# The second state scan issued in pieces between output tiles and weight slots, with GpSimd's two-operand work moved around it

## The chip, the core and the metric

The program runs on one core of a Trainium2 chip. The metric is device microseconds of one execution. The kernel before took 2566.79 us, the median of 3 runs (2566.29 to 2571.04). Engines are named as the profile names them: PE is TensorE, DVE is VectorE, ACT is ScalarE, POOL is GpSimd, SP is SyncE, which issues most DMAs.

## What is computed

One inference step of a two-layer decoder over 304 token columns (a prompt of 16 meta and 256 new tokens, and 8 sample sequences of 4 tokens). Layer 0 is a gated short convolution and a squared-ReLU MLP. Layer 1 is a state space mixer with a gated linear unit (GLU), and another MLP. Only the mixer of layer 1 is touched here:

```python
h_re, h_im = associative_scan(...)          # h[t] = A h[t-1] + B u[t], complex, diagonal
y = einsum(C_re, h_re) - einsum(C_im, h_im) + D * u
g = gelu(y)
out = (g @ w_a) * sigmoid(g @ w_b)          # 2048 x 2048 each
```

## The kernel before, in words

All large products are split into two rounded parts for accuracy: each weight slot of 256 rows x 512 columns is loaded as `raw`, ACT copies it to a rounded part `whi` (L64), and DVE or POOL subtracts to get the rest `wlo` (L66). Three matmuls per pair of tiles follow (L194, L195, L196). A slot is 24 such matmuls. `WeightStream.take` prepares slots two ahead of the one in use; `whi` and `wlo` have 3 buffers each, `raw` has 4. Each slot names the engine that does its L66, "dve" or "pool".

The mixer works on chunks of four tokens. There are 76 chunks (68 of the prompt, 8 of the samples) and 16 channel tiles, in two parts: tiles 0 to 5 (TP1) and tiles 6 to 15 (TP2). For each part the inputs to the states are formed (`m1_run`), then `st_scan` runs the recurrence over the prompt's chunks on DVE, then each tile's output is formed (`y_run`): `st_t` and `st_y` (PE, L1098 and L1107), ACT's copy `vy` (L1112), the transposes of `st_c` (PE, L1123), gelu (ACT, L1126), the rounded part of `g` (ACT, L1129) and the rest (`gt_lo`, POOL, L1130).

`st_scan(1)`, the second scan, has on DVE, in this order:

- 15 steps of four 320-column instructions (L1041, L1042, L1045, L1047), side by side for four blocks of 17 chunks,
- one last step in two shapes, and three carries between blocks (L1060 to L1065),
- six corrections of four 640-column instructions (L1077 to L1080): three for the first half of the states (tiles 6 to 10), then three for the second (tiles 11 to 15).

`st_scan_samples` advances the sample sequences with 8 two-operand instructions on POOL (L1090 to L1093).

The order of the program around it is fixed by the code: the engines' queues are filled in program order. Before: `st_scan(1)` whole, then `y_run(TP1)`, during which slots 0 to 2 are prepared, then four GLU groups of three slots each on tiles 0 to 5 (`group(K1, ...)`, 12 slots, below called slots 0 to 11), then `st_scan_samples(1)`, `y_run(TP2)`, `fin_copy(1)` (POOL gathers the final states, L1220) and the rest of the GLU ("phase 2" below; its first slots are 12, 13, 14). In phase 2, PE transposes the final states (`fin_tr`, L1240) after its fourth slot. The lower parts of slots 0 to 14 are POOL's.

Of the kernel before, what the change touches and what calls it, by code (L numbers as in the profile page):

```python
# [16 lines left out]
P = 128  # L17
D = 2048
DFF = 8192
NT = D // P           # 16 channel tiles  # L20
NK = 76               # 68 prompt chunks of 4 tokens, then 8 sample sequences of 4 tokens
NP = 68
NS = 8
NM = 4                # chunks of meta tokens
NL = NK - NM          # 72 chunks that live on after the state space mixer
N0 = 4 * NK           # 304 columns: column j * 76 + k holds token j of chunk k
N1 = 4 * NL           # 288
# [8 lines left out]
RATE = (2, 0, 0, 2, 3, 3)  # L36


class WeightStream:
    """Weights come in slots of 256 rows x 512 columns; each is split exactly into two float32r parts."""  # L40
# [37 lines left out]
def build(ctx, tc, I, O, dbg=None):  # L78
# [50 lines left out]
    for n, mg in glu[:NPHASE1]:  # L129
        wgroup(I[n][0], K1, mg * 512, "pool")  # L130
# [15 lines left out]
    def later(fn, delay=1, front=False):  # L146
        """front: what frees an accumulator goes before all else"""
        if front:
            i = 0
            while i < len(tasks) and tasks[i][2]:  # L150
                i += 1
            tasks.insert(i, (W.idx + delay, fn, True))
        else:
            tasks.append((W.idx + delay, fn, False))
# [9 lines left out]
    def pop_tasks(n):  # L164
        """second halves of what began at the last call, then one accumulator, then other work"""
        run_pend()
        if tasks and tasks[0][2] and tasks[0][0] <= W.idx:
            tasks.pop(0)[1]()
            if heavy[0]:
                return  # L170
        k = 0
        i = 0
        while i < len(tasks) and k < n:
            if not tasks[i][2] and tasks[i][0] <= W.idx:
                tasks.pop(i)[1]()
                k += 1
            else:
                i += 1
# [7 lines left out]
    def group(kts, rhs, n, rate=1, fast=False):  # L186
        """512 columns of a product: four accumulators; the last one comes late in the first slot"""
        ps = [psum() for _ in range(4)]

        def mm(m, kk, si, hi, lo):  # L190
            xh, xl = rhs(kts[si + kk])
            o = ps[m][:, :n]
            wh, wl = hi[:, kk, m * P:(m + 1) * P], lo[:, kk, m * P:(m + 1) * P]
            T.matmul(out=o, lhsT=wh, rhs=xh, start=si == 0 and kk == 0, stop=False)  # L194
            T.matmul(out=o, lhsT=wh, rhs=xl, start=False, stop=False)  # L195
            T.matmul(out=o, lhsT=wl, rhs=xh, start=False, stop=si + 2 >= len(kts) and kk == 1)  # L196

        for si in range(0, len(kts), 2):
            while si == 0 and len(tasks) > 3 and tasks[3][2]:
                tasks.pop(0)[1]()  # L200
            run_pend()
            hi, lo = W.take()
            if si + 2 >= len(kts):
                order = [(m, kk) for m in range(4) for kk in range(2)]
            else:
                order = [(m, kk) for kk in range(2) for m in range(4 if si else 3)]
                if si == 0:
                    order += [(3, 0), (3, 1)]
            for m, kk in order[:4]:
                mm(m, kk, si, hi, lo)  # L210
            pop_tasks(rate)
            for m, kk in order[4:]:
                mm(m, kk, si, hi, lo)
            if len(tasks) > 5 or fast:
                pop_tasks(rate)
            else:
                run_pend()
            if bg:
                f = bg[0]
                if hasattr(f, "__next__"):  # L220
                    if next(f, bg) is bg:
                        bg.pop(0)
                else:
                    bg.pop(0)
                    if f is not None:
                        it = f()
                        if hasattr(it, "__next__"):
                            bg.insert(0, it)
        return ps

# [21 lines left out]
    def warm_pe(n):  # L252
        """keeps the tensor engine's clock up over a short wait"""
        ps = psum1()
        for _ in range(n):
            T.matmul(out=ps[:, :P], lhsT=ones, rhs=ones, start=True, stop=True)
# [46 lines left out]
    def cols(ap, n):  # L303
        """the last n / 4 chunks of each of the four token rows"""
        v = ap.rearrange("p (j k) -> p j k", j=4)
        return v[:, :, v.shape[2] - n // 4:]
# [29 lines left out]
    def norm_tile(x, t, n, base, eng=None):  # L336
        """square sums and the scaled, split operand of the next product"""
# [4 lines left out]
    def rsqrt_from(ps, s, y, out, then=None):  # L342
        """1 / sqrt(mean + eps): root and reciprocal, then a Newton step"""
# [92 lines left out]
    d_b = dp.tile([2, 64, P, 16], F32, name="d_b")         # ri, p, g, c  # L436
    d_c = dp.tile([2, 64, P, 4, 16], F32, name="d_c")      # ri, p, g, tau, c'
    d_m1 = dp.tile([NT, 2, 64, 4, 2, 64], F32, name="d_m1")  # tile, g2, (j c), q, ri, p
    d_m2 = dp.tile([NT, 2, 64, 4, 2, 64], F32, name="d_m2")  # tile, g2, p, q, ri, (i c')
    d_u = dp.tile([D, N0], F32, name="d_u")  # L440
    d_t = dp.tile([4, 16, P, 4, 16], F32, name="d_t")      # j, c, g, i, c'

    def prep_tasks():
# [27 lines left out]
        def vexp(x, out, ta, tb, tcc):  # L471
            """exp by reduction to |r| <= ln2/2 and a polynomial; x is kept"""
# [15 lines left out]
        # slots of nat: 0 lr, 1 li, 2 log_step, 3 dt, 4..7 temps, 8+2n.. A^(n+1), 16+2n.. E_n  # L488
# [22 lines left out]
        def cmul(o, a, b):  # L511
            """complex product of slot pairs"""
# [29 lines left out]
        def t_wnorm():  # L542
            """the mixer's input weights join B and D"""
# [115 lines left out]
        # local kernels K_tau = Re(C A^tau Bbar), with D on the diagonal of K_0  # L659
# [88 lines left out]
    def taps(t, i):  # L748
        """the convolution over time, scaled by the norm of what it will meet"""
# [87 lines left out]
    def mlp(x, n, base, last_ev):  # L837
        """last_ev(t): what follows once a tile of the residual stream is final"""
# [86 lines left out]
    def u_in(ta, tb):  # L925
        """partition (g2, j, c) of U: token j of a chunk, channel c of every other state group"""
# [30 lines left out]
    def st_m1(t):  # L957
        """inputs to the chunk states, by chunk"""
# [18 lines left out]
    def st_m1t(t):  # L977
        """the same by state, into the scan"""
# [26 lines left out]
    def powers(n):  # L1005
        """A^(4(n+1)) of the block scan's corrections"""
# [14 lines left out]
    def st_scan(pi):  # L1021
        """chunk states: four blocks of 17 chunks side by side, then the carries between them"""
# [13 lines left out]
        def step(items):  # L1036
            """items: previous states, new states (holding the inputs), blocks"""
# [11 lines left out]
        for k in range(1, LBK - 1):  # L1049
            step([(bv[:, :, k], bv[:, :, k + 1], NBK)])  # L1050
        step([(bv[:, 0:3, LBK - 1], bv[:, 1:4, 0], 3), (bv[:, 3:4, LBK - 1], sh[:, NK:NK + 1], 1)])
# [3 lines left out]
        def carry(b):  # L1055
            """i times the carry into block b; the next carry += A^68 times it"""
# [9 lines left out]

        for b in range(1, NBK):
            carry(b)
        n = LBK - 1
        for qa, qb in QCUT[pi]:  # L1070
# [3 lines left out]
            for b in range(1, NBK):  # L1074
# [5 lines left out]
                V.tensor_tensor(out=hb, in0=hb, in1=t2, op=ALU.add)  # L1080

    def st_scan_samples(pi):
        sh = ssm["SH"][pi]
        q0, nq = qrange(pi)
        x, y = (s_[:, 0:NS * nq].rearrange("p (s q) -> p s q", s=NS) for s_ in ssm["st"])
# [29 lines left out]
    def g_at(t):  # L1115
        """rounded and remaining parts of tile t of the mixer's activations, over two buffers"""
        return gh[t // 8][:, t % 8, :], gh[t // 8][:, 8 + t % 8, :]

    def st_c(t):
# [10 lines left out]
        G.tensor_tensor(out=gt_lo, in0=gt[:, :N1], in1=gt_hi.bitcast(F32), op=ALU.subtract)  # L1130
# [5 lines left out]
    # layer 0's MLP, with the transposes of the finished tiles running under its last products  # L1136
# [26 lines left out]
    # rstd in the layout of U: partition (g2, j, c), column k  # L1163
# [24 lines left out]
    st_scan(0)  # L1188
# [3 lines left out]
    st_scan(1)  # L1192
# [9 lines left out]
    def y_run(ts):  # L1202
        ts = list(ts)
        for n, t in enumerate(ts):
# [5 lines left out]
            if 0 < n <= LOOK + 1:  # L1210
                W.prep_to(W.idx + n)
        st_c(ts[-1])

    y_run(TP1)
# [3 lines left out]
    def fin_copy(pi):  # L1218
        q0, nq = qrange(pi)
        G.tensor_copy(out=fin[0].rearrange("p (s r q) -> p s r q", s=9, r=2)[:, :, :, q0:q0 + nq],  # L1220
                      in_=ssm["SH"][pi][:, NK:85])
# [6 lines left out]
    for gi in range(NPHASE1):  # L1228
        ps = group(K1, rhs_g, N1, 0)
        for i in range(4):  # L1230
            S.activation(out=part[:, gi * 4 + i, :], in_=ps[i][:, :N1], func=AF.Copy)
    st_scan_samples(1)
# [15 lines left out]

    fin_copy(1)
# [3 lines left out]
    # gated linear unit  # L1253
# [108 lines left out]
```

## Time and profile before

| What | Value |
|---|---|
| Runs | 2566.29, 2566.79, 2571.04 us |
| Profiled execution, its span | 2566.6 us |
| PE busy | 2458.1 us (96%) |
| DVE busy | 1488.9 us (58%) |
| ACT busy | 967.7 us (38%) |
| POOL busy | 402.1 us (16%) |
| Granted PE clock, mean | 0.982 of full speed |

PE is the busiest engine by far; its 40 slices are full nearly everywhere, with a dip in slice 24 of 40, where the mixer's second part is. The table is an average over stages with different limits. The change lies in the stretch from 1400 to 1600 us of the span, where DVE is at 9 tenths for two slices.

### The profile page before, as it was taken

Reading aid. Unit: us, or ns where it says so; the run is one execution under the profiler, and the core shown is the slowest. Engines: PE = TensorE matmul, PEld = TensorE weight load, DVE = VectorE, ACT = ScalarE, POOL = GpSimd, SP = SyncE. Lnnn points to the kernel's source line nnn. Section 1 sums busy time; section 2 is a strip of 40 time slices with the busy share of each in tenths; the row PEclk is TensorE's granted clock in tenths of the full one; section 3 lists DMA queues with packets and bytes.
Section 4 is the critical chain, followed back from the end, with each engine's and each line's share of the span. In section 5 each row is a group of like instructions: output and inputs, shape, how many; then the busy total and the mean of one; then the engine's idle time right before and its main releaser. Section 6 shows DMA issues by size and latency. Waiting matters only on the chain.

```text
span 2566.6 us, 43303 instructions
## 1 busy us (share of the span) xinstructions
PE 2458.1 (96%) x18078; PEld 2433.9 (95%) x18078; DVE 1488.9 (58%) x1994; ACT 967.7 (38%) x1229; POOL 402.1 (16%) x459
## 2 busy tenths in 40 slices
PE   6999999999989999999989859999999999999998
PEld 5999999998889999999988759999999999999998
DVE  4654556677566675544546992556555545555555
ACT  4333334432334233333324524444333333333334
POOL 2000001025324870000045342000000000000000
PEclk9999999999999999999999979999999999999999
DMA  6555555555656776555569524555555555555554
GB/s 149 156 157 157 160 160 170 158 160 144 164 147 195 221 209 214 158 167 170 159 150 184 153 89 133 165 165 164 166 163 172 161 169 166 165 169 166 165 165 111
DMA packets 256353, 418.17 MB, mean 163 GB/s; under 512 B 64484, under 2 KB 68260, under 8 KB 255980
## 3 DMA queue, kind: packets, MB, share of 16 engines
q1 hardware_dynamic: 248448, 389.62, 52.1%
q0 software_dynamic: 7648, 25.73, 4.8%
q8 instruction: 142, 2.33, 0.4%
q14 instruction: 55, 0.45, 0.0%
q10 hardware_dynamic: 60, 0.05, 0.0%
HBM read 392.71 MB, written 22.63 MB: 162 GB/s over the span
## 4 chain that ended last, share of the span: by engine, by line
PE 59%; DVE 6%; DMA 1%; ACT 0%; issue 0%; SPq 0%; DVEq 0%; ACTq 0%
PE ps L194 19%; PE ps L196 19%; PE ps L195 19%; DVE ssm_tb L1042 1%; PE ps L1107 1%; DVE ssm_tb L1041 1%; DVE ssm_big L1047 1%; DMA raw<-in_mlp_w_down 1%; DVE wlo L66 1%; PE px L684 1%; DVE ssm_big L1045 1%; DMA ssm_xr<-d_u 0%; PE ps L1326 0%; PE ps L1098 0%; ACT whi L64 0%
## 5 line engine op out<-in xcount | busy, mean ns | idle before, releaser
L66 DVE TENSOR_TENSOR wlo<-raw,whi 128x1024 fp32r<-128x1024 f32 x689 | 891.6, 1295 | 931.6 <-ACT whi L64 931.0
L64 ACT ACTIVATE whi<-raw 128x1024 fp32r<-128x1024 f32 x704 | 743.2, 1057 | 1035.9 <-PE ps L195 874.3
L194 PE MATMUL ps<-hid,whi 128*128 128x304 f32 (+1 forms) x2048 | 614.7, 300 | 19.6 <-DVE h L790 17.3
L196 PE MATMUL ps<-hid,wlo 128*128 128x304 f32 (+1 forms) x2048 | 614.2, 300 | 10.2 <-DVE wlo L66 10.2
L196 PE MATMUL ps<-xs_m,wlo 128*128 128x304 f32 (+1 forms) x2048 | 611.8, 299 | 4.2 <-DVE wlo L66 4.2
L195 PE MATMUL ps<-hid,whi 128*128 128x304 f32 (+1 forms) x2048 | 614.0, 300 | 0.0
L194 PE MATMUL ps<-xs_m,whi 128*128 128x304 f32 (+1 forms) x2048 | 611.0, 298 | 0.0
L195 PE MATMUL ps<-xs_m,whi 128*128 128x304 f32 (+1 forms) x2048 | 610.8, 298 | 0.0
L194 PEld LDWEIGHTS ps<-hid,whi 128*128 128x128 f32 x2048 | 388.2, 190 | 22.1 <-DVE h L790 18.7
L196 PEld LDWEIGHTS ps<-hid,wlo 128*128 128x128 f32 x2048 | 388.7, 190 | 11.7 <-DVE wlo L66 11.7
L196 PEld LDWEIGHTS ps<-xs_m,wlo 128*128 128x128 f32 x2048 | 385.3, 188 | 4.9 <-DVE wlo L66 4.9
L195 PEld LDWEIGHTS ps<-hid,whi 128*128 128x128 f32 x2048 | 388.0, 189 | 0.0
L194 PEld LDWEIGHTS ps<-xs_m,whi 128*128 128x128 f32 x2048 | 385.3, 188 | 1.2
L195 PEld LDWEIGHTS ps<-xs_m,whi 128*128 128x128 f32 x2048 | 385.2, 188 | 0.1
L194 PE MATMUL ps<-xs,whi 128*128 128x304 f32 x768 | 233.3, 304 | 5.6 <-DVE h L384 5.6
L196 PE MATMUL ps<-xs,wlo 128*128 128x304 f32 x768 | 233.1, 303 | 0.0
L195 PE MATMUL ps<-xs,whi 128*128 128x304 f32 x768 | 232.6, 303 | 0.0
L728 ACT ACTIVATE hid<-at 128x304 fp32r<-128x304 f32 (+1 forms) x128 | 57.8, 451 | 307.3 <-DVE at L834 307.3
L194 PEld LDWEIGHTS ps<-xs,whi 128*128 128x128 f32 x768 | 145.6, 190 | 5.9 <-DVE h L384 5.8
L196 PE MATMUL ps<-g,wlo 128*128 128x288 f32 x512 | 151.1, 295 | 0.0
L194 PE MATMUL ps<-g,whi 128*128 128x288 f32 x512 | 151.1, 295 | 0.0
L195 PE MATMUL ps<-g,whi 128*128 128x288 f32 x512 | 150.7, 294 | 0.0
(281 smaller groups left out, 2519.4 us busy)
## 6 DMA issues: line engine op xcount, KB each, us to landing
raw<-in_mlp_w_up SPq DMA_DIRECT2D x256, 512.0 KB, 3.8
raw<-in_mlp_w_down SPq DMA_DIRECT2D x256, 512.0 KB, 3.7
raw<-in_conv_w_in SPq DMA_DIRECT2D x96, 512.0 KB, 3.7
raw<-in_conv_w_out SPq DMA_DIRECT2D x32, 512.0 KB, 3.7
raw<-in_ssm_glu_w_b SPq DMA_DIRECT2D x32, 512.0 KB, 3.6
raw<-in_ssm_glu_w_a SPq DMA_DIRECT2D x32, 512.0 KB, 3.8
ssm_big<-d_m SPq DMA_DIRECT2D x64, 128.0 KB, 3.2
d_m<-prep POOLq DMA_DIRECT2D x16, 256.0 KB, 8.9
```

Of the source, the lines that this page charges most:

```text
L64: self.nc.scalar.activation(out=hi, in_=r, func=AF.Copy)
L66: eng.tensor_tensor(out=lo, in0=r, in1=hi.bitcast(F32), op=ALU.subtract)
L194: T.matmul(out=o, lhsT=wh, rhs=xh, start=si == 0 and kk == 0, stop=False)
L195: T.matmul(out=o, lhsT=wh, rhs=xl, start=False, stop=False)
L196: T.matmul(out=o, lhsT=wl, rhs=xh, start=False, stop=si + 2 >= len(kts) and kk == 1)
L684: T.matmul(out=ps[:16, g % 8 * 64:(g % 8 + 1) * 64], lhsT=wl[:, g, :], rhs=cl[:, g, :], start=True, stop=True)
L728: S.activation(out=dh, in_=src, func=AF.Copy)
L1041: V.tensor_tensor(out=u, in0=coef(1, nb), in1=prev[:, :, ::-1, :], op=ALU.mult)
L1042: V.tensor_tensor(out=tr, in0=coef(0, nb), in1=prev, op=ALU.mult)
L1045: V.tensor_tensor(out=dst, in0=dst, in1=u, op=ALU.add)
L1047: V.tensor_tensor(out=dst, in0=dst, in1=tr, op=ALU.add)
L1107: T.matmul(out=ps[:NK, n // 2 * P:(n // 2 + 1) * P], lhsT=ssm["SH"][pi][:, 0:NK, n % 2, tl * 4 + n // 2], rhs=ssm["m2"][t % 3][:, n, :], s ...
```

## The change

`st_scan` becomes a generator that stops after each step, after the last step, after the carries, and after each correction: 15 + 1 + 1 + 6 = 23 pieces. The first scan is run through at once, as before. The second is advanced by one piece before `y_run(TP1)`, by 2, 1, 1, 1, 1, 1 pieces after the output tiles 0 to 5 (`YUNITS`), and by one piece in each of the 12 slots (`PUNITS`); the remaining three run before `y_run(TP2)`. The lower parts of slots 0 to 11 move from POOL to DVE, and so do the `gt_lo` of tiles 0 to 5. The lower parts of slots 12, 13 and 14 stay on POOL. `fin_copy(0)` moves from POOL to ACT. `st_scan_samples(1)` moves from before `y_run(TP2)` to behind it, ahead of `fin_copy(1)`, with its scratch in another tile. Comments are removed.

```diff
+YUNITS = (2, 1, 1, 1, 1, 1)
+PUNITS = 1
...
 for n, mg in glu[:NPHASE1]:
-    wgroup(I[n][0], K1, mg * 512, "pool")
+    wgroup(I[n][0], K1, mg * 512)
...
             pop_tasks(rate)
+            if each is not None:
+                each()
             for m, kk in order[4:]:
...
         for k in range(1, LBK - 1):
             step([(bv[:, :, k], bv[:, :, k + 1], NBK)])
+            yield
...
+        yield
         for b in range(1, NBK):
             carry(b)
+        yield
...
                 V.tensor_tensor(out=hb, in0=hb, in1=t2, op=ALU.add)
+                yield
+
+    def advance(n):
+        for _ in range(n):
+            next(scan1, None)
...
-        x, y = (s_[:, 0:NS * nq].rearrange("p (s q) -> p s q", s=NS) for s_ in ssm["st"])
+        st = ssm["st"] if pi == 0 else [ssm["xr"][:, 2304 + i * 320:2624 + i * 320] for i in range(2)]
+        x, y = (s_[:, 0:NS * nq].rearrange("p (s q) -> p s q", s=NS) for s_ in st)
...
-        G.tensor_tensor(out=gt_lo, in0=gt[:, :N1], in1=gt_hi.bitcast(F32), op=ALU.subtract)
+        eng = V if t < PARTS[0] else G
+        eng.tensor_tensor(out=gt_lo, in0=gt[:, :N1], in1=gt_hi.bitcast(F32), op=ALU.subtract)
...
-    st_scan(1)
+    scan1 = st_scan(1)
+    advance(1)
...
+            if n < len(units):
+                advance(units[n])
         st_c(ts[-1])
 
-    y_run(TP1)
+    y_run(TP1, YUNITS)
...
+        if pi == 0:
+            S.activation(out=dst, in_=src, func=AF.Copy)
+        else:
+            G.tensor_copy(out=dst, in_=src)
...
-        ps = group(K1, rhs_g, N1, 0)
+        ps = group(K1, rhs_g, N1, 0, each=lambda: advance(PUNITS))
...
-    st_scan_samples(1)
+    for _ in scan1:
+        pass
...
+    st_scan_samples(1)
     fin_copy(1)
```

The order of the instructions on each engine, as it is built, shows what moved. On DVE, in the middle of `y_run(TP1)`, a row is a line, an operation, output and inputs, and a shape. Before, one step of the second scan follows the other:

```order
L1047 TENSOR_TENSOR ssm_big<-ssm_big,ssm_tb 128x4x80
L1041 TENSOR_TENSOR ssm_tb<-a_77,ssm_big 128x320
L1042 TENSOR_TENSOR ssm_tb<-a_77,ssm_big 128x320
L1045 TENSOR_TENSOR ssm_big<-ssm_big,ssm_tb 128x4x80
L1047 TENSOR_TENSOR ssm_big<-ssm_big,ssm_tb 128x4x80
```

Now, at the same place, `gt_lo` of an output tile (L1145) and the lower part of a slot (L68) stand between two steps (L1045 to L1051):

```order
L1051 TENSOR_TENSOR ssm_big<-ssm_big,ssm_tb 128x4x80
L1145 TENSOR_TENSOR g_14164<-gt,g_14164 128x288
L68 TENSOR_TENSOR wlo<-raw,whi 128x1024
L1045 TENSOR_TENSOR ssm_tb<-a_77,ssm_big 128x320
L1046 TENSOR_TENSOR ssm_tb<-a_77,ssm_big 128x320
L1049 TENSOR_TENSOR ssm_big<-ssm_big,ssm_tb 128x4x80
L1051 TENSOR_TENSOR ssm_big<-ssm_big,ssm_tb 128x4x80
```

So six `gt_lo` and three lower parts are put into the scan here.

On DVE, at the end of the four GLU groups on tiles 0 to 5: before, the third carry is followed by the first correction.

```order
L1060 TENSOR_SCALAR ssm_tb<-ssm_big 128x40
L1061 COPY ssm_tb<-ssm_big 128x40
L1062 TENSOR_TENSOR ssm_tb<-ssm_tb,ssm_big 128x80
L1063 TENSOR_TENSOR ssm_tb<-ssm_tb 128x80
L1064 TENSOR_TENSOR ssm_big<-ssm_big,ssm_tb 128x80
L1065 TENSOR_TENSOR ssm_big<-ssm_big,ssm_tb 128x80
L1077 TENSOR_TENSOR ssm_tb<-ssm_tb,ssm_big 128x640
L1078 TENSOR_TENSOR ssm_tb<-ssm_tb 128x640
L1079 TENSOR_TENSOR ssm_big<-ssm_big,ssm_tb 128x32x20
L1080 TENSOR_TENSOR ssm_big<-ssm_big,ssm_tb 128x32x20
```

Now the lower part of slot 11, the last one that DVE does here, stands between them:

```order
L1065 TENSOR_SCALAR ssm_tb<-ssm_big 128x40
L1066 COPY ssm_tb<-ssm_big 128x40
L1067 TENSOR_TENSOR ssm_tb<-ssm_tb,ssm_big 128x80
L1068 TENSOR_TENSOR ssm_tb<-ssm_tb 128x80
L1069 TENSOR_TENSOR ssm_big<-ssm_big,ssm_tb 128x80
L1070 TENSOR_TENSOR ssm_big<-ssm_big,ssm_tb 128x80
L68 TENSOR_TENSOR wlo<-raw,whi 128x1024
L1084 TENSOR_TENSOR ssm_tb<-ssm_tb,ssm_big 128x640
L1085 TENSOR_TENSOR ssm_tb<-ssm_tb 128x640
L1086 TENSOR_TENSOR ssm_big<-ssm_big,ssm_tb 128x32x20
L1087 TENSOR_TENSOR ssm_big<-ssm_big,ssm_tb 128x32x20
```

The six corrections stand behind it without a break, so that between the lower parts of slots 10 and 11 DVE has the carries, and behind the latter only corrections.

On POOL, from the last tiles of `y_run(TP1)` to `y_run(TP2)`, before:

```order
L1130 TENSOR_TENSOR g_14164<-gt,g_14164 128x288 x3
L1220 COPY ssm_xr<-ssm_xr 128x18x24
L66 TENSOR_TENSOR wlo<-raw,whi 128x1024 x11
L1090 TENSOR_TENSOR ssm_tb<-a_77,ssm_big 128x320
L1091 TENSOR_TENSOR ssm_tb<-a_77,ssm_big 128x320
L1092 TENSOR_TENSOR ssm_tb<-ssm_tb 128x320
L1093 TENSOR_TENSOR ssm_big<-ssm_big,ssm_tb 128x8x40
```

Now, in the whole stretch from the first scan to phase 2 (L1145 is `gt_lo`, L1104 to L1107 the samples):

```order
L68 TENSOR_TENSOR wlo<-raw,whi 128x1024 x2
L1145 TENSOR_TENSOR g_14164<-gt,g_14164 128x288 x2
L1145 TENSOR_TENSOR g_14872<-gt,g_14872 128x288
L68 TENSOR_TENSOR wlo<-raw,whi 128x1024
L1145 TENSOR_TENSOR g_14872<-gt,g_14872 128x288 x7
L1104 TENSOR_TENSOR ssm_xr<-a_77,ssm_big 128x320
L1105 TENSOR_TENSOR ssm_xr<-a_77,ssm_big 128x320
L1106 TENSOR_TENSOR ssm_xr<-ssm_xr 128x320
L1107 TENSOR_TENSOR ssm_big<-ssm_big,ssm_xr 128x8x40
```

Two lower parts (slots 12 and 13) are what POOL has left before the tiles of TP2; the samples' eight instructions now stand between the last `gt_lo` and `fin_copy(1)`. The orders on PE and SP are the same as before.

## Rows read from the trace of the kernel before

**Rows 1.** Waits of PE over the whole span: what waited, for whom, us, times, longest

```profile
PE ps L1107 <- DVE ssm_big L1080: 28.1, 1, 28.1
...
PE ps L1107 <- issue: 7.3, 1, 7.3
```

**Rows 2.** PE in order of time: start, us, line, operation, [idle before <- releaser]

```profile
1464.18 0.38 PE L194 MATMUL ps<-g,whi 128*128 128x288 f32 x1
...
1502.47 1.03 PE L1098 MATMUL ps<-ssm_big,ssm_xr 128*76 128x128 f32 x8
1531.59 2.63 PE L1107 MATMUL ps<-ssm_big 128*76 128x128 f32 x11 [28.09 <-DVE ssm_big L1080]
```

**Rows 3.** DVE in order of time, 1451 to 1541: the second scan

```profile
1451.04 0.48 DVE L1041 TENSOR_TENSOR ssm_tb<-a,ssm_big 128x320 f32<-128x320 f32 x1
...
1454.74 1.02 DVE L1041 TENSOR_TENSOR ssm_tb<-a,ssm_big 128x320 f32<-128x320 f32 x1
1455.68 2.65 DVE L1042 TENSOR_TENSOR ssm_tb<-a,ssm_big 128x320 f32<-128x320 f32 x1
...
1511.83 0.49 DVE L1041 TENSOR_TENSOR ssm_tb<-a,ssm_big 128x320 f32<-128x320 f32 x1
...
1517.39 0.41 DVE L1041 TENSOR_TENSOR ssm_tb<-a,ssm_big 128x240 f32<-128x240 f32 x1
...
1531.45 0.82 DVE L1077 TENSOR_TENSOR ssm_tb<-ssm_tb,ssm_big 128x640 f32<-128x640 f32 x1
...
1539.90 0.83 DVE L1080 TENSOR_TENSOR ssm_big<-ssm_big,ssm_tb 128x640 f32<-128x640 f32 x1
```

**Rows 4.** POOL grouped by line and shape, 1451.04 to 1531.45: xcount, busy, mean ns

```profile
L66 POOL TENSOR_TENSOR wlo<-raw,whi 128x1024 fp32r<-128x1024 f32 x14 | 35.9, 2565 | 5.9 <-ACT whi L64 5.6
L1130 POOL TENSOR_TENSOR g<-gt,g 128x288 fp32r<-128x288 f32 x6 | 6.0, 1008 | 37.7 <-DMA ssm_big<-d_m 37.7
L1091 POOL TENSOR_TENSOR ssm_tb<-a,ssm_big 128x320 f32<-128x320 f32 x2 | 2.2, 1101 | 0.0
```

**Rows 5.** DVE in order of time, 1580 to 1600: work of phase 2, alone

```profile
1580.08 1.22 DVE L66 TENSOR_TENSOR wlo<-raw,whi 128x1024 fp32r<-128x1024 f32 x1 [2.35 <-ACT whi L64]
1581.22 0.45 DVE L1261 TENSOR_TENSOR ssm_xr<-ssm_xr,ps 128x288 f32<-128x288 f32 x1
```

**Rows 6.** ACT in order of time, one slot's rounded part

```profile
1499.39 1.06 ACT L64 ACTIVATE whi<-raw 128x1024 fp32r<-128x1024 f32 x1 [2.12 <-PE ps L195]
```

**Rows 7.** Stretches: length, busy of PE, PEld, DVE, ACT, POOL, then granted PE clock

```profile
1438.00:1445.20 7.20, 0.00 (x0) 0.01 (x1) 7.00 (x20) 0.00 (x0) 0.00 (x0) 0.67 0.56 124
1445.20:1447.00 1.80, 1.77 (x9) 1.80 (x10) 1.76 (x4) 0.00 (x0) 0.00 (x0) 0.50 0.99 308
...
1457.00:1464.00 7.00, 6.58 (x57) 6.43 (x56) 6.93 (x5) 4.93 (x10) 7.00 (x5) 1.00 0.52 116
```

**Rows 8.** Chain of waits in order of time: start, us, what

```profile
1435.75 0.20 issue
...
1531.59 3.70 PE ps L1107 x16
1535.28 1.32 PE ps L1098 x8
1536.60 2.11 PE ps L1107 x16
...
1538.98 0.88 PE ps L1098 x8
...
1565.87 0.18 PE ps L194
...
1577.04 0.44 PE px L1240 x4
```

**Rows 9.** POOL in order of time, around phase 2's start

```profile
1549.94 0.80 POOL L1130 TENSOR_TENSOR g<-gt,g 128x288 fp32r<-128x288 f32 x1
...
1567.70 0.78 POOL L1220 COPY ssm_xr<-ssm_big 128x720 f32<-128x720 f32 x1
```

More of the change, by code (lines that the diff above doesn't have):

```diff
@@ L184, in flush, with group @@
                 tasks.pop(0)[1]()
-    def group(kts, rhs, n, rate=1, fast=False):
+    def group(kts, rhs, n, rate=1, fast=False, each=None):
         ps = [psum() for _ in range(4)]
@@ L1187, in build @@
     m1_run(TP1, side)
-    st_scan(0)
+    for _ in st_scan(0):
+        pass
     m1_run(TP2, [])
@@ L1200, in build, with y_run @@
     W.dma_to(W.idx + NRAW)
-    def y_run(ts):
+    def y_run(ts, units=()):
         ts = list(ts)
@@ L1219, in fin_copy @@
         q0, nq = qrange(pi)
-        G.tensor_copy(out=fin[0].rearrange("p (s r q) -> p s r q", s=9, r=2)[:, :, :, q0:q0 + nq],
-                      in_=ssm["SH"][pi][:, NK:85])
+        dst, src = fin[0].rearrange("p (s r q) -> p s r q", s=9, r=2)[:, :, :, q0:q0 + nq], ssm["SH"][pi][:, NK:85]
+        if pi == 0:
+            S.activation(out=dst, in_=src, func=AF.Copy)
+        else:
+            G.tensor_copy(out=dst, in_=src)
     fin_copy(0)
@@ L1228, in build @@
     for gi in range(NPHASE1):
-        ps = group(K1, rhs_g, N1, 0)
+        ps = group(K1, rhs_g, N1, 0, each=lambda: advance(PUNITS))
         for i in range(4):
             S.activation(out=part[:, gi * 4 + i, :], in_=ps[i][:, :N1], func=AF.Copy)
-    st_scan_samples(1)
+    for _ in scan1:
+        pass
     gh[1] = rp.tile([P, NT, N1], F32R, tag="HID", name="g1", bufs=2)
```

## The prediction

> **What bounds the kernel now.** I read the waits of PE over the whole span first, since PE is busy for 96% of it: the one long wait in the mixer is L1107 (the output of the first tile of the second part) for DVE's L1080, 28.1 us, once, beside one of 7.3 us ahead of the first tile [rows 1]. PE in order of time places it: the 12 slots on tiles 0 to 5 run from 1464.18 to 1502.47, that is 38.29 / 12 = 3.19 us a slot; then PE does `st_t` of tile 6 and stands still until 1531.59 [rows 2]. So DVE's second scan ends last there, and every microsecond by which its third correction comes earlier is a microsecond of the span, until PE itself is late.
>
> DVE in order of time tells why the scan is long. It starts at 1451.04; the third correction ends at 1531.45 (the fourth starts there), the sixth ends at 1540.73 [rows 3]. PE started 0.14 us behind the third, not behind the sixth. In that stretch a step's instruction takes 0.49 us alone and 2.65 us when a lower part runs on POOL; beside a `gt_lo` it takes 1.02 us [rows 3]. Grouped by line, POOL has 14 lower parts of 2.57 us, 6 `gt_lo` of 1.01 us and 8 instructions of the samples of about 1.1 us there [rows 4].
>
> **The scan without POOL.** Three steps take 1517.39 - 1511.83 = 5.56 us, so one takes 1.85; the last step, carries and first three corrections take 1531.45 - 1517.39 = 14.06 [rows 3]. Alone, the scan up to PE's release is 15 x 1.85 + 14.06 = 41.9 us; it took 80.4. The 38.5 us between are explained by POOL: a lower part adds 2.65 - 0.49 = 2.16, 14 of them 30.2; `gt_lo` 6 x 0.53 = 3.2; the samples 8 x 0.64 (one of DVE's finishes per POOL instruction of 1.10, for 1.85 / 4 = 0.46 alone) = 5.1; together 38.5. So I trust the price of 2.16 us for each lower part left on POOL.
>
> **What the change does to DVE.** Removed from POOL in this stretch: 12 lower parts, 6 `gt_lo`, the samples, and one copy that goes to ACT (ACT is busy for 4.9 of 7 us in 1457 to 1464 [rows 7], so I take some 0.6 us there as hidden; if it were not, it would delay one rounded part by 0.6 us that is needed two slots later). Added to DVE: 12 lower parts at 1.14 us each (start to start, 1580.08 to 1581.22 [rows 5]) = 13.7, and 6 `gt_lo` of 288 columns, which I take at 0.40 (0.45 for the 288-column L1261 less the 0.08 by which neighbours overlap [rows 5]; bounds 0.3 to 0.6) = 2.4. Left on POOL inside the scan: the lower parts of slots 12 and 13. They need their rounded part, which ACT makes in 1.06 us when PE has left slots 9 and 10 [rows 6], so they come when DVE is at the carries, slot 11's lower part or the first correction: 2 x 2.16 = 4.3 us more. Sum: 1451.04 + 41.9 + 13.7 + 2.4 + 4.3 = 1513.3, PE 0.1 later: **1513.4 instead of 1531.59, 18.2 us earlier.**
>
> Bounds of those two: 0 (they fall beside nothing) and 4.3. I take 4.3, since every one of the 14 before cost its price. The Trainium skill's SBUF — State Buffer page (Who interferes with whom) says that of DVE with two SBUF inputs and a GpSimd instruction the one that starts first holds the shared ports, and that "Issue order, not op shape, decides who blocks". By that rule alone DVE might lose nothing here, with PE at 1509.1; the rows show POOL getting in between any two of DVE's instructions, so the sum stays.
>
> **Is PE late then, or starved?** DVE passes 8 pieces, 6 `gt_lo` and 3 lower parts by 1451.04 + 14.8 + 2.4 + 3.4 = 1471.6. The last `gt_lo` (tile 5) is needed in slot 2, which starts at 1464.18 + 2 x 3.19 = 1470.6 and wants tile 5 some 0.4 us later: a stall of about 0.7 us. From there a slot gives DVE one lower part and one piece, 1.14 + 1.85 = 2.99 us, against PE's 3.19: DVE keeps ahead by 0.2 a slot. Slot 11's lower part stands behind the carries (2.9 us, within the 14.06) and meets slot 12's on POOL, so it ends near 1502.0, while PE is ready for it at about 1500.0. PE then leaves slot 11 at 1505.2 and `st_t` of tile 6 (1.0 us [rows 2]) at 1506.2, and waits 7.2 us for 1513.4. The stalls within the slots are all inside this wait and cost nothing; with the first stall alone PE would be free at 1504.2. So DVE still ends last, and the wait of 28.1 us becomes one of about 7.
>
> **The clock.** After the wait of 28.1 us before, 16 L1107 and 8 L1098 took 3.70 + 1.32 us, then 2.11 + 0.88: 2.0 us lost [rows 8]. After 7.2 us of idleness at 1438 the granted clock was 0.50 too, which is 1.2 GHz [rows 7]. A wait of 7 us should thus cost the same 2.0 us, so I give no gain for it; a wait well under that might give it back.
>
> **What is late next.** The samples' 8 instructions now stand before `fin_copy(1)` on POOL, and PE's transposes of the final states wait for that copy in PE's queue, with phase 2's matmuls behind them. Before, the copy ended at 1567.70 + 0.78 = 1568.48, and PE came to the transposes at 1577.04: 8.6 us of slack [rows 8, 9]. The samples take 8 x 1.1 = 8.8 us at the price beside DVE [rows 4], or 8 x 0.89 = 7.1 from the 0.80 of 288 columns alone [rows 9]. The stall is 0 to 0.7 us; I take 0.2. Slot 14's lower part stands behind `gt_lo` of tile 8 in both orders. The fourth to sixth correction (9.3 us, and a `gt_lo` beside them) are needed by tile 11, five tiles or 16 us behind tile 6, so they stay hidden. The orders of SP and PE do not move, and a raw buffer is freed by DVE at most some 3 us later than POOL freed it, with four slots in flight; the transfers stay hidden.
>
> From L1107's start to phase 2's start PE took 1565.87 - 1531.59 = 34.3 us [rows 8], and I leave that as it is. **Sum:** 2566.6 - 18.2 + 0.2 = 2548.6 us of span. The median of the runs stands 0.2 above the profiled span (2566.79), so I predict **2548.8 us**.
>
> **Rivals.**
>
> 1. POOL's two lower parts cost nothing, and PE waits only 5 us: 18.2 + 4.3 = 22.5 earlier, 2544.5; with the clock kept besides, 2542.5. For it: whether one meets a correction depends on tenths of a microsecond. Against: DVE is never idle there. Chance 0.14.
> 2. Handing over costs. Each of 18 foreign instructions (12 lower parts, 6 `gt_lo`) is a place where DVE may stand for a signal; a bare gap of issue in the first scan was 0.20 us [rows 8]. 18 x 0.2 = 3.6, so 2552.4; then DVE takes 3.2 to 3.4 a slot and paces PE. For it: the margin is 0.2 us a slot. Against: what each of them waits for is done one to two slots earlier. Chance 0.14.
> 3. The change doesn't release PE early: PE waits for the last of all pieces rather than the third correction. Then 9.3 us are lost again: 2558.1. Against: PE started 0.14 us behind the third before [rows 2, 3]. Chance 0.05.
> 4. Slower than before: the stalls that DVE now puts between slots bring PE's clock to 1.2 GHz in the GLU groups. A slot would take 6.4 us, 12 of them 76.6 from 1464.2, to 1540.8, and `st_y` of tile 6 would start near 1542, 10 us later than before: 2577. It decides from the point where 9 of the 12 slots run at half speed (9 x 3.19 = 28.7, the wait it would use up). For it: the clock did fall in idle stretches [rows 7]. Against: with PE idle for 0.42 of 7.00 us at 1457 the granted clock was 1.00 [rows 7], and my stalls are below 2 us. Chance 0.03.
>
> **How the numbers follow.** The forecast (2546.5 to 2551) has 0.62, the rivals 0.14, 0.14, 0.05 and 0.03, and 0.02 is left for no change. A measurement of this kernel can tell 0.2%, or 5.1 us, from no change: faster means below 2561.7. Forecast and rivals 1, 2 and 3 lie below it, 0.95; within 0.2% 0.02, slower 0.03. The range takes in rivals 1 and 2: 2543.5 to 2554.5.
>
> **What would show it.** Right: PE's wait for the corrections falls from 28.1 to about 7 us; the scan's instructions are near 0.49 us except for two of some 2.6 beside POOL's slots 12 and 13; L1107 starts near 1513; phase 2 starts near 1548; the transposes wait under 1 us for the copy. Wrong: waits of PE for `wlo` in most slots (rival 2), L1107 released by the sixth correction (3), a granted clock under 1.00 in the slots (4), or a time above 2555, which would mean a cost that no row here shows.

## The result and the profile after

The changed kernel takes **2551.03 us** (median of 4 runs, 2549.1 to 2553.18) against 2568.31 for the kernel before in the same comparison: a ratio of 0.9934, 95% interval 0.9922 to 0.9946. In a second comparison, on another chip, it was 2549.47, ratio 0.9928 [0.9915, 0.994]. 2548.8 had been predicted, 18.0 us below before; the medians differ by 17.3 and 18.1. So the time lies inside the stated range (2543.5 to 2554.5), a hair beyond the bounds of the forecast itself (2546.5 to 2551). The profiled execution took 2551.72, its span is 2549.9. Line numbers have moved: L66 is now L68, L64 L66, L1041 to L1047 are L1045 to L1051, L1077 to L1080 are L1084 to L1087, L1098 L1112, L1107 L1121, L1220 L1243, L1240 L1263.

The waits of PE over the whole span, the view of [rows 1]:

```profile
PE ps L1121 <- issue: 14.7, 2, 7.4
...
PE px L1263 <- POOL ssm_xr L1243: 1.5, 1, 1.5
...
PE ps L1121 <- DVE ssm_tb L1045: 1.0, 1, 1.0
```

The row of 28.1 us behind DVE is gone. The 7.3 of "issue" ahead of the first tile stands as before, and a second one of 7.4 has come beside it: it is what is left of the 28.1. PE in order of time shows where, the answer to [rows 2]:

```profile
1505.93 1.04 PE L1112 MATMUL ps<-ssm_big,ssm_xr 128*76 128x128 f32 x8
1514.38 3.67 PE L1121 MATMUL ps<-ssm_big 128*76 128x128 f32 x16 [7.41 <-issue]
```

"issue" names no releaser, but DVE in order of time does: tile 6's products start 0.19 us behind the start of the fourth correction (0.14 before). The scan, the answer to [rows 3]:

```profile
1453.64 0.48 DVE L1045 TENSOR_TENSOR ssm_tb<-a,ssm_big 128x320 f32<-128x320 f32 x1
...
1454.96 0.49 DVE L1051 TENSOR_TENSOR ssm_big<-ssm_big,ssm_tb 128x320 f32<-128x320 f32 x1
1455.49 0.49 DVE L1045 TENSOR_TENSOR ssm_tb<-a,ssm_big 128x320 f32<-128x320 f32 x1
...
1459.09 0.45 DVE L1145 TENSOR_TENSOR g<-gt,g 128x288 fp32r<-128x288 f32 x1
1459.45 1.22 DVE L68 TENSOR_TENSOR wlo<-raw,whi 128x1024 fp32r<-128x1024 f32 x1
...
1475.10 1.22 DVE L68 TENSOR_TENSOR wlo<-raw,whi 128x1024 fp32r<-128x1024 f32 x1
1476.24 0.49 DVE L1045 TENSOR_TENSOR ssm_tb<-a,ssm_big 128x320 f32<-128x320 f32 x1
...
1477.56 0.49 DVE L1051 TENSOR_TENSOR ssm_big<-ssm_big,ssm_tb 128x320 f32<-128x320 f32 x1
1477.97 1.22 DVE L68 TENSOR_TENSOR wlo<-raw,whi 128x1024 fp32r<-128x1024 f32 x1
...
1499.45 1.22 DVE L68 TENSOR_TENSOR wlo<-raw,whi 128x1024 fp32r<-128x1024 f32 x1
1500.59 0.82 DVE L1084 TENSOR_TENSOR ssm_tb<-ssm_tb,ssm_big 128x640 f32<-128x640 f32 x1
1501.32 3.03 DVE L1085 TENSOR_TENSOR ssm_tb<-ssm_tb 128x640 f32<-128x640 f32 x1
1504.28 3.00 DVE L1086 TENSOR_TENSOR ssm_big<-ssm_big,ssm_tb 128x640 f32<-128x640 f32 x1
...
1514.19 0.82 DVE L1084 TENSOR_TENSOR ssm_tb<-ssm_tb,ssm_big 128x640 f32<-128x640 f32 x1
```

A slot is one lower part and one step, 1475.10 to 1477.97 = 2.87 us. Only two instructions of the scan are long, and POOL in the same stretch names the cause, its two lower parts inside the scan, where [rows 4] had 14 (the third row is slot 14's, behind the scan):

```profile
1500.77 2.90 POOL L68 TENSOR_TENSOR wlo<-raw,whi 128x1024 fp32r<-128x1024 f32 x1 [81.26 <-ACT whi L66]
1503.95 2.65 POOL L68 TENSOR_TENSOR wlo<-raw,whi 128x1024 fp32r<-128x1024 f32 x1 [0.28 <-ACT whi L66]
...
1529.97 2.35 POOL L68 TENSOR_TENSOR wlo<-raw,whi 128x1024 fp32r<-128x1024 f32 x1
```

Stretches, as [rows 7]: the slots, the wait, and tile 6 behind it.

```profile
1466.00:1506.00 40.00, 39.58 (x303) 39.43 (x302) 39.48 (x83) 19.71 (x32) 4.96 (x2) 1.00 0.58 177
1506.97:1514.38 7.41, 0.01 (x2) 0.04 (x1) 7.31 (x11) 0.00 (x0) 0.00 (x0) 0.78 0.31 88
1514.38:1516.00 1.62, 1.62 (x8) 1.62 (x9) 1.62 (x3) 0.00 (x0) 0.00 (x0) 0.50 0.00 0
...
1518.00:1519.00 1.00, 1.00 (x11) 1.00 (x10) 1.00 (x3) 0.59 (x1) 0.00 (x0) 1.00 0.00 0
```

PE and DVE are both busy for 99% of the slots, at the full clock.

**How the runs are compared.** The second scan begins at 1449.06 to 1453.64 in the profiles of this study; in two profiles of the changed kernel it begins at 1453.64 and 1451.67. Nothing that was edited stands ahead of it, so this is scatter, as large as some effects below. Each run is therefore cut at two marks: *a* from the scan's first instruction to tile 6's first L1121, *b* from there to the span's end. *c* is the part of *b* up to the last norm (the wait of PE that is L1315 before, L1339 after, and L1339 to L1352 in the experiments). The experiments further below are in the same table.

| Run | scan starts | a | b | c | a + b | median, us |
|---|---|---|---|---|---|---|
| before | 1451.04 | 80.55 | 1035.0 | 1016.4 | 1115.6 | 2568.31 |
| after | 1453.64 | 60.74 | 1035.5 | 1017.7 | 1096.3 | 2551.03 |
| after, again (experiment 12) | 1451.67 | 60.73 | 1035.3 | 1017.4 | 1096.0 | 2549.47 |
| experiment 1 | 1450.83 | 75.64 | 1035.9 | 1018.3 | 1111.6 | 2565.49 |
| experiment 2 | 1449.06 | 96.18 | 1035.8 | 1016.3 | 1131.9 | 2584.07 |
| experiment 3 | 1450.21 | 58.60 | 1036.3 | 1018.3 | 1094.9 | 2546.45 |
| experiment 4 | 1451.19 | 64.59 | 1034.5 | 1016.3 | 1099.1 | 2551.52 |
| experiment 5 | 1452.50 | 60.72 | 1034.2 | 1016.4 | 1094.9 | 2550.99 |
| experiment 6 | 1453.07 | 60.76 | 1034.7 | 1016.7 | 1095.4 | 2545.97 |
| experiment 7 | 1452.48 | 56.33 | 1046.9 | 1028.9 | 1103.2 | 2556.47 |
| experiment 8 | 1452.82 | 53.14 | 1050.9 | 1032.4 | 1104.1 | 2557.83 |
| experiment 9 | 1453.28 | 56.33 | 1037.1 | 1017.8 | 1093.4 | 2546.57 |

So *a* fell by 19.8, *b* rose by 0.5, and the profiled run began the scan 2.6 later: 16.7 us between the two profiled spans.

What follows *c*, the last norm and the output, is edited nowhere, and it takes 17.7 to 19.5 us in these profiles. Changed kernel and experiment 9 at that place, first PE's wait that ends *c*, then the stretch of the 64 transposes behind it:

```profile
2532.11 0.65 PE L1339 MATMUL ps<-one,acc 128*72 128x1 f32 x8 [1.67 <-DVE acc L324]
2532.63:2539.79 7.16, 7.16 (x67) 6.89 (x65) 5.91 (x12) 5.15 (x9) 0.00 (x0) 1.00 0.42 85
```

```profile
2527.46 0.65 PE L1342 MATMUL ps<-one,acc 128*72 128x1 f32 x8 [1.67 <-DVE acc L325]
2527.98:2536.80 8.82, 8.82 (x67) 8.09 (x65) 6.04 (x12) 5.39 (x9) 0.00 (x0) 0.81 0.38 77
```

The same transposes took 1.66 us longer at a granted clock of 0.81 on the mean. Differences of *b* are therefore read from *c*.

### The profile page after: what moved, and what is told of

The parts are those of the page before. It is cut to its first block, busy times and chain, and to the rows that moved or that the text cites. A ratio compares the mean times of both kernels' runs of the same rounds, so it can differ in the third digit from the quotient of the medians.

```text
span 2549.9 us, 43295 instructions
## 1 busy us (share of the span) xinstructions
PE 2457.9 (96%) x18078; PEld 2433.5 (95%) x18078; DVE 1469.3 (58%) x2012; ACT 968.1 (38%) x1230; POOL 369.6 (14%) x440
## 4 chain that ended last, share of the span: by engine, by line
PE 58%; DVE 2%; DMA 1%; issue 1%; POOL 0%; ACT 0%; DVEq 0%; ACTq 0%; POOLq 0%
PE ps L196 18%; PE ps L198 18%; PE ps L197 18%; PE ps L1121 1%; DMA raw<-in_mlp_w_down 1%; PE px L688 1%; PE ps L1112 0%; DMA ssm_big<-d_m 0%; DVE ssm_tb L1045 0%; PE ps L1350 0%; DVE wlo L68 0%; DVE ssm_xr L1051 0%; DVE ssm_tb L1046 0%; DVE ssm_xr L1049 0%; PE ps L969 0%
## 5 line engine op out<-in xcount | busy, mean ns | idle before, releaser
L68 DVE TENSOR_TENSOR wlo<-raw,whi 128x1024 fp32r<-128x1024 f32 x701 | 908.7, 1297 | 934.2 <-ACT whi L66 933.5
L66 ACT ACTIVATE whi<-raw 128x1024 fp32r<-128x1024 f32 x704 | 743.2, 1057 | 1034.4 <-PE ps L197 874.7
```

What stands on the lines that cost most here:

```text
L66: self.nc.scalar.activation(out=hi, in_=r, func=AF.Copy)
L68: eng.tensor_tensor(out=lo, in0=r, in1=hi.bitcast(F32), op=ALU.subtract)
```

## The experiments

**1 and 2. One part of the change at a time.** The pieces alone, with POOL's work as before (but the samples behind `y_run(TP2)`):

```diff
-        wgroup(I[n][0], K1, mg * 512)
+        wgroup(I[n][0], K1, mg * 512, "pool")
...
-        eng = V if t < PARTS[0] else G
+        eng = G
...
-        if pi == 0:
+        if False:
```

> The scan stays in pieces, but the lower parts of slots 0 to 11, gt_lo of tiles 0 to 5 and the first copy of final states are POOL's again. Theory (the scan is its own 41.9 us plus 2.2 us for each lower part that POOL runs beside it, and PE waits for its third correction): 41.9 + 14 x 2.16 + 6 x 0.53 = 75.3 us from the scan's start to PE's release, against 80.4 before and 60.6 in the changed kernel; PE waits about 22 us; time about 2566. Rival (issuing in pieces alone is what gains): 60 us, time about 2551.

2565.49 us, ratio 0.9992 [0.9983, 1.0001]; a = 75.64 (75.3 expected). The 4.9 us less than before are put down to the samples, which no longer run beside the scan (5.1 by the prediction's price); so by this run some 4.9 of the 19.8 us by which *a* fell in the changed kernel belong to them, and 14.9 to the work that went to DVE. The medians don't show the 4.9: the interval of the ratio reaches 1, and *c* is 1.9 longer than before, which holds a wait of 1.5 for the copy of the final states as in the changed kernel. The longest wait in the stretch:

```profile
PE ps L1121 <- DVE ssm_big L1087: 22.8, 1, 22.8
```

The engines alone, with the scan whole ahead of `y_run(TP1)`:

```diff
-    advance(1)
+    advance(99)
```

> The engines are as in the changed kernel, but the second scan is issued whole ahead of the output tiles. Theory: the scan then takes its own 51 us, and every gt_lo and lower part stands behind it on DVE; ACT's gelu of tile 2 waits for the gt_lo of tile 0, so slot 0 starts about 56 us after the scan's start instead of about 13, and tile 6's output some 40 us after that, without a wait for the scan. About 32 us slower than the changed kernel: 2583, slower than before. Rival (taking the work off POOL alone is what gains): 2551 or less.

2584.07 us (2583 expected), ratio 1.0061 [1.0044, 1.0079]: slower than before. The scan now runs without POOL and ends by 1500.24, but the first `gt_lo` stands behind all of it in DVE's queue. ACT waits for that (first row, waits of ACT), and PE for ACT's copy (second row, waits of PE):

```profile
ACT gt L1140 <- DVE g L1145: 45.3, 2, 45.1
```

```profile
PE ps L1137 <- ACT vy L1126: 42.5, 3, 41.6
```

Neither part makes the kernel measurably faster by itself. Here DVE could take POOL's work only when the scan could be interrupted for it, and interrupting the scan gained nothing while POOL stretched it. The first copy of final states on ACT (0.55 us there) was not tried alone.

**3. The two lower parts left on POOL.**

```diff
-        wgroup(I[n][0], K2[:6], mg * 512, "pool" if first else "dve")
+        wgroup(I[n][0], K2[:6], mg * 512, "dve")
```

> The changed kernel with the lower parts of slots 12, 13 and 14 on DVE instead of POOL. Theory: each of the two that fall into the corrections costs DVE 1.14 us instead of 2.2, so PE's release comes 58.5 us after the scan's start instead of 60.6; time about 2549. Rival (what POOL does beside the corrections is hidden): no change, or 2.3 us more for the two added on DVE.

2546.45 us, ratio 0.9916 [0.99, 0.9933]; a = 58.60. Two lower parts of 1.14 on DVE in place of two of 2.2 lost to POOL: 4.4 - 2.3 = 2.1, and *a* is 2.1 shorter. This settles rival 1: what POOL kept did cost its price. *c* is 0.6 longer: behind a wait of 6.05 us PE was slow for longer than behind 7.41 (last section).

**4 and 5. The clock behind the wait.** Filler matmuls ahead of `y_run(TP2)`, 54 and then 30:

```diff
     for _ in scan1:
         pass
+    warm_pe(54)
```

> The changed kernel with 54 matmuls of 128 columns on constants in PE's queue ahead of the second part's tiles, where PE stands idle for 7.4 us. Theory (the idle wait costs 2.0 us of half clock behind it): the granted clock stays at 1.00, the 16 L1121 of tile 6 take 2.1 us instead of 3.67, time about 2549. Rival (the slow first tile is not the clock's): still 3.67, time 2551; or PE comes out late by the filler's own length, above 2551.

> As the run with 54 filler matmuls, with 30: a filler takes 12.2 / 54 = 0.226 us there, so 30 take 6.8 of the 7.4 us for which PE stands idle. Theory: clock kept at 1.00, the 16 L1121 of tile 6 in 2.1 us, PE released as in the changed kernel 60.7 us after the scan's start, and the tiles behind it 1.5 to 2.0 us earlier; time about 2549. Rival: the clock falls in spite of it and the first 16 take 3.67.

With 54: 2551.52 us, ratio 0.9939 [0.9924, 0.9954]; with 30: 2550.99, 0.9936 [0.9921, 0.9951]. PE in order of time with 54, then with 30:

```profile
1502.85 12.22 PE L260 MATMUL px<-ones 128*128 128x128 f32 x108
1514.90 1.04 PE L1112 MATMUL ps<-ssm_big,ssm_xr 128*76 128x128 f32 x8
1515.78 2.27 PE L1121 MATMUL ps<-ssm_big 128*76 128x128 f32 x16
```

```profile
1504.26 6.86 PE L260 MATMUL px<-ones 128*128 128x128 f32 x60
1510.95 1.04 PE L1112 MATMUL ps<-ssm_big,ssm_xr 128*76 128x128 f32 x8
1513.22 2.35 PE L1121 MATMUL ps<-ssm_big 128*76 128x128 f32 x16 [1.23 <-issue]
```

A filler makes two records and takes 12.22 / 54 = 0.226 us. The 54 ended past DVE's release (1511.75 in that run), so *a* was 64.6 and the fillers themselves were the wait. The 30 fit (*a* = 60.72) and tile 6 ran at full clock, 2.35 instead of 3.67, so *c* is 1016.4 in place of 1017.7. 1.3 us is less than the medians can tell here; only the local reading shows it.

**6. The samples spread over tiles 11 to 14**, two of the eight instructions in each:

```diff
+            if side is not None and n > 4:
+                next(side, None)
+                next(side, None)
```

> The changed kernel with the samples' eight POOL instructions in pairs between the tiles 11 to 15 instead of behind the last one. Theory: the copy of the final states comes about 8 us earlier against phase 2, the 1.5 us for which PE's transposes waited for it are gone, nothing else moves: time about 2549.5. Rival: gt_lo of these tiles comes late behind them, gelu and the copy of y wait in turn, and PE loses more than 1.5 us between the tiles.

2545.97 us, ratio 0.992 [0.9905, 0.9934]. What it removes is seen on POOL of the changed kernel, in order of time:

```profile
1550.06 0.89 POOL L1104 TENSOR_TENSOR ssm_xr<-a,ssm_big 128x320 f32<-128x320 f32 x1
...
1552.82 1.74 POOL L1107 TENSOR_TENSOR ssm_big<-ssm_big,ssm_xr 128x320 f32<-128x320 f32 x1
...
1556.44 1.74 POOL L1106 TENSOR_TENSOR ssm_xr<-ssm_xr 128x320 f32<-128x320 f32 x1
...
1559.20 1.66 POOL L1243 COPY ssm_xr<-ssm_big 128x720 f32<-128x720 f32 x1
```

Three of these nine instructions are 0.87 longer than their like, where phase 2's lower parts on DVE (1552.48, 1555.67, 1558.84) meet them. With the samples spread, the copy follows the last `gt_lo` and takes 0.78:

```profile
1550.23 0.78 POOL L1251 COPY ssm_xr<-ssm_big 128x720 f32<-128x720 f32 x1
```

PE's wait of 1.5 is gone, and *c* is 1.0 shorter (*a* 60.76); part of the 1.5 went to the clock, which was low for longer behind tile 6's wait than in the changed kernel's profile (last section). The median's gain over the changed kernel is larger than that, but the intervals of the two ratios overlap.

**7 and 8. Preparing slots 12 to 14 later.** `plimit` stops the preparation at 12 slots until the scan is through, and the lower parts of slots 12 to 14 go to DVE as in experiment 3; in the second of these the samples are spread as well, and the corrections are cut into 12, 12 and 16 columns, so that tile 6 needs only the first twelve:

```diff
-        while self.nprep < min(n, self.limit):
+        while self.nprep < min(n, self.limit, self.plimit):
...
+    W.plimit = W.idx + 12
...
     for _ in scan1:
         pass
+    W.plimit = len(slots)
...
-    QCUT = [((0, 12), (12, 24)), ((0, 20), (20, 40))]
+    QCUT = [((0, 12), (12, 24)), ((0, 12), (12, 24), (24, 40))]
```

> The changed kernel with slots 12, 13 and 14 prepared only between the tiles of the second part, on DVE, behind the whole scan: nothing runs on POOL beside the corrections and nothing is added between them. Theory: 56.2 us from the scan's start to PE's release, 4.4 less than in the changed kernel and 2.3 less than with these lower parts between the corrections; PE's wait falls to about 3 us; time about 2546.5, or 2 less if the clock survives a wait of 3 us. Rival: the late preparation makes PE wait at slot 12 for its lower part, and the 4.4 us come back there.

> Late preparation of slots 12 to 14 and the samples between the tiles, and besides the corrections in three parts (tiles 6 to 8, 9 to 11, 12 to 15) instead of two. Theory: three corrections of 384 columns instead of 640 end about 3.2 us earlier, 53 us after the scan's start, which is when PE is through with slot 11 and the next tile's first product; PE does not wait there at all, the clock stays, the copy is early: about 11 us less than the changed kernel, 2540. Rival: a later part of the corrections becomes the wait (tile 9 or tile 12), or PE's own queue is the end and the gain stops at about 6 us, 2545.

Both expectations failed: 2556.47 us, 0.9956 [0.9939, 0.9972], and 2557.83, 0.9961 [0.9946, 0.9976]. Up to tile 6 they did as expected (a = 56.33 and 53.14). Then *b* was 1046.9 and 1050.9. The chain of waits of the first of them:

```profile
1520.15 1.05 ACT whi L67
1521.22 1.24 DVE wlo L69
1522.48 0.37 SPq L56
1522.90 0.59 SPq L956
...
1524.85 3.85 DMA ssm_big<-d_m
1528.84 3.67 PE ps L1122 x16
```

and SP's queue in that run:

```profile
1495.42 24.62 SPq L56 DMA_DIRECT2D raw<-in_ssm_glu_w_b  x3
```

The loads of later slots were still issued early. Those of slots 16 and 17 need the raw buffers of slots 12 and 13, which are freed by those slots' lower parts, and these were now put off. The loads stood at the head of SP's queue, with the tiles' loads of `tt` and `m2` (L956, L952) behind them. PE ran dry three tiles later, for 8.8 and 15.1 us.

**9. The same, with those loads held.**

```diff
-        while self.ndma < min(n, self.limit):
+        while self.ndma < min(n, self.limit, self.plimit + NRAW):
```

> As e4_defer (lower parts of slots 12 to 14 made behind the scan, on DVE), but the loads of the slots from 16 on are held until the lower part of slot 12 is issued, so that SP's queue has none that waits ahead of the second part's m2 and tt loads. If e4_defer lost its 10 us to that load at the head of SP's queue (24.6 us in its trace), PE's wait of 8.8 us for m2 is gone, tile 6's products start 56.3 us after the scan's start as there, and from the scan's start to the span's end it takes 56.3 + 1035.0 = about 1091 us (e4_defer 1103.2, after 1096.3): some 2545 us. Rival: the late preparation itself is what costs (rounded and lower parts late for slot 12); then the time stays near 2556.

2546.57 us, ratio 0.9915 [0.9899, 0.993]: 9.9 below experiment 7, by one line. PE's wait of 8.8 for `m2` is gone; a = 56.33, b = 1037.1. So the cause was SP's queue, and not the late preparation. That *b* is still 1.6 above the changed kernel's comes from the kernel's end, where the clock was lower in this profile: *c* is only 0.1 above.

**10 to 12. Put together, and the changed kernel again on the same chip.** First: experiment 3, the samples spread, the corrections in three parts. Second: that with the deferral and the held loads.

> The change with the three lower parts of POOL on DVE, the corrections cut into 12, 12 and 16 columns, and the samples in pairs between tiles; nothing deferred. Tile 6 then needs three corrections of 2.0 us (e7_thirds) in place of three of 3.07: with the two or three lower parts of 1.14 among them PE starts tile 6 some 55.5 us after the scan's start (e8_tail_dve 58.4, after 60.7) and stands for about 3 us; no wait at the last part's transposes (1.5). Scan start to span end about 1090 (after 1096.3), some 2542 us. Rival: the shorter pieces cost more than they give (more instructions, more waits of DVE for ACT's rounded parts): not below e8_tail_dve's 2546.

> e11_thirds_dve with the preparation of slots 12 to 14 behind the scan and the loads held as in e10_hold. Tile 6 starts 53.1 us after the scan's start, as in e7_thirds, with PE idle 0.4 us and no clock loss in tile 6; no wait for m2 and none at the last transposes. From tile 6 to the end 1035.5 - 2.0 - 1.5 = 1032: scan start to span end about 1085 us, some 2538 us, 13 below the change. If instead a wait for a weight slot or a load appears behind the tiles, it stays above 2545.

> The changed kernel itself, on the same chip as the other three, so that they can be set against it: 2551 us by its first runs, a ratio of 0.993 to before.

| Kernel | median (range), us | ratio to before | a | b | c |
|---|---|---|---|---|---|
| after, again | 2549.47 (2544.19 to 2552.38) | 0.9928 [0.9915, 0.994] | 60.73 | 1035.3 | 1017.4 |
| thirds, nothing deferred | 2542.51 (2540.81 to 2543.78) | 0.9901 [0.9887, 0.9914] | 55.40 | 1033.4 | 1014.6 |
| thirds, deferred, loads held | 2537.24 (2535.25 to 2541.82) | 0.9883 [0.987, 0.9897] | 53.14 | 1032.5 | 1014.6 |

All three came out as expected: 2542 and 2538 us had been said for the two new ones, 55.5 and 53.1 for their *a*. The last is the fastest kernel of the study: 12.2 us below the changed kernel on that chip, with ranges that do not meet. PE hardly stands still ahead of tile 6:

```profile
1503.90 2.35 PE L1126 MATMUL ps<-ssm_big 128*76 128x128 f32 x16 [0.82 <-issue]
```

## Why the prediction was right

- **The scan without POOL.** Right, and its size nearly so: 62.4 us from the scan's start to tile 6 was predicted, 60.74 measured. POOL's two lower parts cost 3.03 + 3.00 - 2 x 0.82 = 4.4 (predicted 4.3). A lower part on DVE took 1475.10 to 1476.24, 1.14, as taken. The 1.6 us too many lie in the steps. A step takes 1.85 when another step follows: the next one's first instruction, which reads what this one's last wrote, starts 0.53 behind it (1454.96 to 1455.49). With a lower part or a `gt_lo` behind it, that distance is 0.41 (1477.56 to 1477.97), and the step takes 1476.24 to 1477.97 = 1.73. 13 of the 15 steps have one: 1.6 us.
- **PE's wait** came out right, 7.4 for 7.2, by luck: two errors cancel. DVE was 1.6 early, and PE was 1.9 earlier than predicted, at 53.3 us behind the scan's start instead of 55.2. Of the stalls that had been put between the slots, 0.7 at slot 2 and 2.0 at slot 11, neither came: the 12 slots took 1467.65 to 1506.10, 3.20 us each. Slot 11's lower part started at 45.8 and met nothing of POOL's, which fell on the first correction. Slot 0 in turn began 14.0 us behind the scan's start, 0.9 later than before: PE had waited 1.0 ahead of tile 2 (third row of its waits above).
- **The clock.** Right in kind: 0.50 behind the wait. Tile 6's products and the next eight took 3.67 + 0.90, 1.6 more than 2.11 + 0.88, where 2.0 had been taken from [rows 8]; against experiment 5, where the clock stayed, it is 1.3.
- **What is late next.** The right place, the wrong size: PE waited 1.5 us for the copy, where 0.2 was taken and 0.7, for which no working is given, was the bound. The samples and the copy took 10.8 us, from 1550.06 to 1560.86, not 7.9 to 9.6. The prediction had a price for samples beside DVE, 1.1 us each, but from the scan's short instructions; here they stood at 0.88 except where one of phase 2's lower parts on DVE held POOL up, 0.87 more for each of three. That had no term in the sum. So *c* rose by 1.3: the 1.5 for the copy, less what PE's slow stretch behind tile 6 was shorter than before.
- **The total** is nearer than its parts: *a* fell by 19.8 (18.2 said) and *c* rose by 1.3 (0.2 said), so the two misses nearly cancel, 18.5 us together against 18.0.
- **The rivals.** 1: experiment 3 excludes it. 2: there are no gaps; DVE is busy for 39.48 of 40 us in the slots. 3: PE follows the third correction. 4: the clock is 1.00 in the slots. What would have made it slower was another thing, shown by experiment 2: the same engines without the pieces.

The Trainium skill's SBUF — State Buffer page (SBUF: two separate sides) has the port pair that DVE and GpSimd share held for the whole instruction by whichever starts first. The rows agree in both directions: POOL's first lower part, recorded from 1500.77, is 2.90 long against 2.35 at 1529.97, and began in the middle of a DVE instruction of 0.82; the next DVE instruction then took 3.03. The reading weighed ahead of the result, that a DVE which issues first might lose nothing, is not borne out: both times POOL came in between two of DVE's back-to-back instructions.

Open: the medians of experiments 3 and 6, which lie 3 to 5 us below the changed kernel's where a + b is 1.4 and 0.9 lower. The intervals of their ratios, 0.99 to 0.9933 and 0.9905 to 0.9934, overlap with the changed kernel's, so the excess is not shown to be more than scatter. What made PE wait for 1.0 us ahead of tile 2 in the changed kernel was not followed up.

## What to carry to other kernels

Where one engine's long sequence holds up the busiest engine, look for two things at once: who stretches its instructions, and what would stand behind it if it took that work over. Here only both together paid. Before a preparation is put off, ask which DMA waits for the buffer that it frees, and what stands behind that DMA in its queue.

## What the runs showed that was not expected

- **Loads that waited at the head of SP's queue held up those behind them**: 9.9 us, from two loads that nobody needed yet.
- **PE's idle time ahead of tile 6 and its clock behind it.** From tile 6's first product to tile 7's first it is 3.05 to 3.06 us in experiments 5, 8, 10 and 11, where PE had been idle for 1.23, 0.41, 2.69 and 0.82: the clock was at 1.00, 2.4 GHz. Idle for 3.47 and 3.62 (experiments 9 and 7): 4.31 and 4.52. Idle for 6.05 to 28.09 (before, after, experiments 1, 3, 6 and 12): 4.10 to 5.17, with the clock at 0.50, 1.2 GHz, at first. The two profiles of the changed kernel alone give 4.40 behind 7.41 us and 4.10 behind 7.64. The stretches of experiment 9, tile 6's products and the eight behind them, and of experiment 10:

```profile
1509.61:1512.20 2.59, 2.59 (x16) 2.59 (x17) 2.56 (x4) 0.00 (x0) 0.00 (x0) 0.79 0.00 0
1512.20:1513.90 1.70, 1.70 (x10) 1.70 (x9) 1.70 (x3) 0.59 (x1) 0.00 (x0) 0.50 0.04 10
```

```profile
1505.59:1507.70 2.11, 2.11 (x16) 2.11 (x17) 2.08 (x5) 0.00 (x0) 0.00 (x0) 1.00 0.74 208
```

  So cutting that wait from 7.4 to 2.7 us or less gives back, beside its own length, the 1.0 to 1.3 us by which PE was slow behind it. Cutting it to 3.5 gave nothing of that back: 4.31 against 4.40 and 4.10.
